# The values of a gated recurrence: turned in 32 by 32 blocks by VectorE when projected, and stored as rows of tokens

## The chip, the cores and the metric

The kernel runs on one core of one Trainium2 chip. The metric is the device time of one execution in microseconds. Each version is run several times on the chip and the median is given; one further execution is recorded by the hardware profiler.

## What is computed

One layer of a hybrid decoder: width 1024, a sequence of 1024 tokens behind 16 learned meta tokens (1040 in all), everything in fp32. In the reference:

```python
h = h + 0.5 * swiglu(rms_norm(h, ffn1_norm), ffn1_w_in, ffn1_w_out)
u = rms_norm(h, mix_norm) @ w_in
hq, hf, hi, hg, sq, sk, sv = split(u)
o_hg = hgrn2(hq, hf, hi, hg, lb, hgrn_out_norm)      # 4 heads, keys and values of 128
o_sb = stick_breaking(sq, sk, sv, sb_q_norm, sb_k_norm)  # 8 heads of 64
h = h + concat(o_hg, o_sb) @ w_out
h = h + 0.5 * swiglu(rms_norm(h, ffn2_norm), ffn2_w_in, ffn2_w_out)
```

The change concerns `hgrn2`, a recurrence over tokens with a matrix S as its state in each head:

```python
# S_t = diag(f_t) S_{t-1} + (1 - f_t) i_t^T ;  o_t = S_t^T q_t ;  y = RMSNorm_head(o) * silu(g)
f = lb + (1 - lb) * sigmoid(f_raw);  k = (1 - lb) * sigmoid(-f_raw);  q = silu(q_raw);  v = i_raw
# in blocks of 128 tokens: scores inside a block, the state between blocks
```

The value v (the i of the formula) enters in two places: in the product of the scores inside a block with v, and in the update of the state, keys by v. Both sum over tokens.

## The kernel before

**Layout.** Activations are kept turned: the features lie on the partitions, the tokens along the row. Matmuls with weights are made of three products of high and low fp32r parts (`product`, lines 243 to 254), so that a step of `wo` or `proj` is a triple of matmuls of lines 250, 251 and 252.

**The recurrence's columns.** `hgrn_fill` (line 1085) projects, for each of the 4 heads, the columns of v, f, q and g in this order (line 1079). For v and f the tokens are cut in the four pieces of `PIECES` (line 31), for q and g in two halves. A piece is taken out of PSUM by `use` (line 1093): for v by a copy on ScalarE into a staging tile (line 1101; four tiles `st` take turns, line 1091), for f by two sigmoids on ScalarE and two operations on VectorE (1103 to 1109), for q and g by a sigmoid and a product (1112, 1113). Then SP stores the tile in DRAM (`hg_v`, `hg_f`, `hg_k`, `hg_q`, `hg_g`; lines 1110 and 1114), each with features as rows and tokens along the row. Of v, f and q the second half of the tokens is stored in reversed order.

A first part of these columns is woven into the projections of the stick-breaking heads; 76 steps are spread by `braid` (line 1609) over the stick-breaking attention (scores, log-weights `wu` and `wm` subtracted on VectorE at line 1535, TensorE transposes of them through `flip` at line 1417); what is left runs beside the first pieces of the heads.

**The heads.** `hgrn_attend` (line 1138) is a generator, one for each head; each `yield` gives the planner a cost on TensorE and a wait. Its pieces are:

- loads from DRAM (lines 1149 to 1152): vT first (the whole v of the head, 128 by 1040), then KB, QA, F and the meta parts KM and FM; the decay products over 1, 2, 4 ... 64 tokens on GpSimd (line 1168);
- nine transposes on TensorE of vT, through `flip` (lines 1172 to 1176): one of the 16 meta tokens, copied to vm by VectorE, and two groups of four blocks of 128, each copied to vr by ScalarE. vr and vm have tokens on the partitions, as the products with v want them;
- the scores KB by QA inside blocks (line 1187), the diagonal taken out by VectorE (1189), QA multiplied by F (1190);
- seven levels (line 1204), each with a copy of KB to KP on ScalarE (1208), a product on TensorE into the banks `lvl` (1213), its selection into `attn` (VectorE's copy_predicated at 1220 for the first five, ScalarE copies at 1230 for the last two), and two pairs of products with the decays on VectorE (1243);
- the transposes of the keys (1248 and 1255, `km` and `knp`), copied out to kms and kn; kn lies in vT's tile. Then the load of g into KB's tile (1258);
- the state: `s` (1262), seven products `up` of kn and vr (1269), and the chain over blocks on VectorE (1272). km, knp, s, up and the later `onp` share two PSUM banks (`tr`);
- the outputs `op` (1282, 1286), their norm (squares on ScalarE 1291, root 1293, reciprocal and product on VectorE 1294 to 1296, the product written into kn), and the transposes back `onp` (1302), gated by g (1305) and split in high and low parts `oH` (1310, 1311).

Tiles of a head have three buffers each, so head 3 reuses those of head 0: its loads wait until head 0 has let them go.

**Order.** TensorE's order is written by hand, by `weave` (line 1639): it keeps a clock, adds the costs that the generators and the fill give, and takes a head's next piece when its wait has passed. The fill is first the rest of the columns, beside which only the first pieces of heads 0 to 2 run (line 2123), then `mix_out` (1579), the products of the stick-breaking half of o with w_out (`wo`), which need oT, loaded at line 2151, and the weights wh and wl, loaded at line 221. There are three lanes: heads 0 and 3, head 1, head 2 (2176, 2177). The order on VectorE, ScalarE and SP is decided by the scheduler.

Of the kernel before, what the change touches and what calls it, by code (L numbers as in the profile page):

```python
# [11 lines left out]
F32 = mybir.dt.float32  # L12
# [8 lines left out]
P = 128  # L21
D = 1024
KT = D // P
SEQ = 1024
META = 16
T = META + SEQ
# [1 line left out]
EPS = 1e-6  # L28
HALVES = [(META, 512), (META + 512, 512)]
CHUNKS = [(META + 512, 512), (0, 264), (264, 264)]  # L30
PIECES = [(0, 264), (264, 264), (528, 256), (784, 256)]
LEVELS = [1, 2, 4, 8, 16, 32, 64]
NEG = -1e30

# [6 lines left out]
class Block:  # L41
# [1043 lines left out]
    def hgrn_fill(self, xh, xl, pool, dst):  # L1085

        nc = self.nc
        plan, cols = self.heads_plan, self.columns_of_heads()

        def staged(n):  # L1090
            return pool.tile([P, 512], F32, tag="st", name="st", bufs=4)[:, :n]

        def use(kind, h, ps, c0, n):
            s = slice(c0, c0 + n) if kind in "vf" else slice(c0 - META, c0 - META + n)
            t = staged(n)
            if c0 >= HALVES[1][0] and kind != "g":
                ps = ps[:, ::-1]
                at = s.start + HALVES[1][0] + T - 2 * c0 - n
                s = slice(at, at + n)
            if kind == "v":  # L1100
                nc.scalar.copy(t, ps)
            elif kind == "f":
                k = staged(n)
                nc.scalar.activation(t, ps, AF.Sigmoid)
                nc.scalar.activation(k, ps, AF.Sigmoid, scale=-1.0)
                nc.vector.tensor_scalar(
                    t, t, self.lbc[:, h : h + 1], self.lb[:, h : h + 1], ALU.mult, ALU.add
                )
                nc.vector.tensor_scalar_mul(k, k, self.lbc[:, h : h + 1])
                nc.sync.dma_start(dst["k"][h, :, s], k)  # L1110
            else:
                nc.scalar.activation(t, ps, AF.Sigmoid)
                nc.vector.tensor_mul(t, t, ps)  # L1113
            nc.sync.dma_start(dst[kind][h, :, s], t)

        def weights(i):
            return self.col_tile(self.a["w_in"][0], cols[i])

        kept = {"next": None}

        def part(i, ci, c0, n, half):
            if ci == 0 and half == 0:
                kept["w"] = kept["next"] or weights(0)
                kept["next"] = weights(i + 1) if i + 1 < len(plan) else None
            if half == 0:
                kept["ps"] = self.proj_bank(n)
            self.product(
                kept["ps"], kept["w"], xh, xl, c0, n, range(4 * half, 4 * half + 4)
            )
            if half == 1:  # L1130
                use(*plan[i], kept["ps"], c0, n)

        for i, (kind, _) in enumerate(plan):
            for ci, (c0, n) in enumerate(PIECES if kind in "vf" else HALVES):
                for half in range(2):
                    yield 12 * (n * 0.42 + 13), lambda a=(i, ci, c0, n, half): part(*a)

    def hgrn_attend(self, h, pool, src, oH):
# [3 lines left out]
        nc = self.nc  # L1142

        def tile_of(name, n):
            return pool.tile([P, n], F32, tag=name, name=name, bufs=3)

        QA, KB, F, vT = (tile_of(x, n) for x, n in (("QA", SEQ), ("KB", SEQ), ("F", SEQ), ("vT", T)))
        KM, FM, TM = (tile_of(x, META) for x in ("KM", "FM", "TM"))
        for t, x in ((vT, src["v"][h]), (KB, src["k"][h][:, META:]), (QA, src["q"][h]),
                     (F, src["f"][h][:, META:]), (KM, src["k"][h][:, :META]),  # L1150
                     (FM, src["f"][h][:, :META])):
            nc.sync.dma_start(t, x)
        vr = tile_of("vr", SEQ).rearrange("p (c d) -> p c d", d=P)
# [4 lines left out]
        vm, kms = (  # L1158
            pool.tile([META, P], F32, tag=x, name=x, bufs=3) for x in ("vm", "kms")
        )  # L1160
        ss, sq = tile_of("ss", 8), tile_of("sq", P)
        where = [0, 1, 2, 3, 7, 6, 5, 4]
        decays, at = [F], 0
        for n in LEVELS:
            nb = 512 // (2 * n)
# [2 lines left out]
            nc.gpsimd.tensor_mul(decays[-1], tk[:, :, 0], tk[:, :, 1])  # L1168
            at += 2 * nb
        yield 0, 4000  # L1170

        ps = self.flip(vT, [(0, META)])
        nc.vector.tensor_copy(vm, ps[:META, 0, :])
        for q in range(2):
            ps = self.flip(vT, [(META + (4 * q + j) * P, P) for j in range(4)])
            nc.scalar.copy(vr[:, 4 * q : 4 * q + 4, :], ps)
        yield 960, 500

        def strided(x, offset, *dims):
            y = x[:, offset:]  # L1180
            return bass.AP(y.tensor, y.offset, [list(d) for d in (y.ap[0], *dims)])

        for half in range(2):
            ps = self.pz.tile([P, 4, P], F32, tag="z", name="lvl")
            for j in range(4):
                c = slice((4 * half + j) * P, (4 * half + j + 1) * P)
                nc.tensor.matmul(ps[:, j, :], KB[:, c], QA[:, c], start=True, stop=True)
            m = self.ident.unsqueeze(1).broadcast_to([P, 4, P])
# [46 lines left out]
        for i, n in enumerate(LEVELS):  # L1235
            level(i, n)
            nb = 512 // (2 * n)
            for eng, x, x0, x1, t0, t1 in (
# [3 lines left out]
                y = strided(x, x0, (x1, 2), (2 * n, nb), (1, n))  # L1242
# [4 lines left out]
        km = self.ptr.tile([P, P], F32, tag="tr", name="km")  # L1247
        nc.tensor.transpose(km[:META, :], KM, self.ident)
        nc.vector.tensor_copy(kms, km[:META, :])
        kn = vT[:, :SEQ].rearrange("p (c d) -> p c d", d=P)  # L1250
        for q in range(2):
            ps = self.ptr.tile([P, 4, P], F32, tag="tr", name="knp")
            for j in range(4):
                s = (4 * q + j) * P
# [6 lines left out]
        ps = self.ptr.tile([P, P], F32, tag="tr", name="s0")  # L1261
        nc.tensor.matmul(ps, kms, vm, start=True, stop=True)
        nc.vector.tensor_copy(S[:, 0, :], ps)
        for q in range(2):
            ps = self.ptr.tile([P, 4, P], F32, tag="tr", name="up")
            js = [j for j in range(4) if 4 * q + j < 7]
            for j in js:
                c = where[4 * q + j]
                nc.tensor.matmul(ps[:, j, :], kn[:, c, :], vr[:, c, :], start=True, stop=True)
            for j in js:  # L1270
                c = 4 * q + j
# [27 lines left out]
        for half, on in enumerate(outs):  # L1299
            ps = self.ptr.tile([P, 4, P], F32, tag="tr", name="onp")  # L1300
            for j in range(4):
                nc.tensor.transpose(ps[:, j, :], on[:, j, :], self.ident)
            t = attn[half].rearrange("p c t -> p (c t)")
            ps = ps.rearrange("p j t -> p (j t)")
# [383 lines left out]
    def run(self):  # L1688
        nc, tc, a = self.nc, self.tc, self.a
# [20 lines left out]
        with ExitStack() as c0:  # L1710
            with ExitStack() as c1:
# [121 lines left out]
                with tc.manual_schedule(engines={nc.tensor.engine}), ExitStack() as c2:  # L1833
# [46 lines left out]
                    v = [nc.vector] * 2  # L1880
# [204 lines left out]
                with tc.manual_schedule(engines={nc.tensor.engine}):  # L2085
# [20 lines left out]
                    for i, n in enumerate(LEVELS[:5]):  # L2106
                        m = self.masks[:, i, :].rearrange("p (b h r) -> p b h r", h=2, r=n)
# [30 lines left out]
            with tc.manual_schedule(engines={nc.tensor.engine}), ExitStack() as cx:  # L2138
                with ExitStack() as c1:
# [100 lines left out]
                r = self.inv_rms_rows(sums[1], n, px, ppb)  # L2240
# [55 lines left out]
```

## Time and profile before

| | us |
|---|---|
| median of 3 runs | 2004.04 |
| lowest and highest run | 2003.74, 2004.24 |
| the profiled execution, device time | 2002.59 |
| its span in the profile | 2000.7 |
| granted TensorE clock, mean | 0.999 of full speed |

How to read the lines below. Times are in microseconds unless marked ns. PE is TensorE's matmuls, PEld its weight loads (beside PE), DVE is VectorE, ACT ScalarE, POOL GpSimd, SP the engine that issues most DMAs (SPq its queue). L1176 is line 1176 of the kernel before. `out<-in` are the program's names of tiles. A row of a timeline gives start, duration, engine, line, operation, tiles, shapes and count, and in square brackets how long the engine had been idle before, and what ended that. A row of the chain gives start, duration and what ran: the chain is followed back from the last instruction, at each step to what released it. In groups by line, the number after the bar is busy time, then the mean of one in ns, then the engine's idle time just before these instructions with its releasers. Waits are listed as: who <- on what, sum in us, times, longest. DMA rows give the count, the size and the median time from issue to landing. Where a row has three numbers with slashes, they are the least, the median and the greatest duration in ns, followed by the starts of the first and the last.

### The profile page before, as it was taken

What the parts mean: (1) busy time and instruction counts of PE and PEld (TensorE: products, weight loads), DVE (VectorE), ACT (ScalarE), POOL (GpSimd) and SP (SyncE); (2) the same over time, 40 slices, a digit from 0 to 9 for tenths busy, and PEclk for the clock granted to TensorE, in tenths of its full rate; (3) what the DMA queues carried; (4) which work ended last, traced back from release to release, by engine and by line L of the source; (5) the groups of instructions that cost most, each with busy time, mean ns of one, the idle gap of its engine ahead of it and who ended that gap; (6) DMA issues with size and microseconds to landing.
All of it is one profiled execution on the core that took longest, in us unless ns stands there. A gap on an engine that the chain in (4) does not pass through costs nothing.

```text
span 2000.7 us, 30716 instructions
## 1 busy us (share of the span) xinstructions
PE 1956.6 (98%) x10940; PEld 1646.5 (82%) x10940; DVE 1362.6 (68%) x2140; ACT 860.7 (43%) x1731; POOL 455.3 (23%) x604
## 2 busy tenths in 40 slices
PE   7999999999999999999999999999999999999998
PEld 6788888888888888888888978877888888888887
DVE  7977777876677752247777767557566767767774
ACT  6523443334444544456666635433132332344443
POOL 3010100010000003233333331320544644520000
PEclk9999999999999999999999999999999999999999
DMA  7256787758965226445454166665523323268463
GB/s 211 87 160 170 250 269 248 242 184 314 381 197 185 95 88 182 142 137 132 121 149 121 56 254 174 167 223 171 193 95 111 106 95 111 100 262 305 118 199 137
DMA packets 315576, 347.16 MB, mean 174 GB/s; under 512 B 61520, under 2 KB 216656, under 8 KB 315424
## 3 DMA queue, kind: packets, MB, share of 16 engines
q1 hardware_dynamic: 297136, 292.18, 46.5%
q0 software_dynamic: 17248, 53.03, 7.7%
q8 instruction: 86, 1.41, 0.3%
q14 instruction: 66, 0.54, 0.1%
q10 hardware_dynamic: 1040, 0.00, 0.0%
HBM read 233.75 MB, written 111.38 MB: 173 GB/s over the span
## 4 chain that ended last, share of the span: by engine, by line
PE 91%; DVE 4%; DMA 2%; ACT 1%; issue 1%; POOL 0%; SPq 0%; DVEq 0%; ACTq 0%
PE o L723 21%; PE qb L450 17%; PE qc L450 12%; PE qa L450 12%; PE proj L250 5%; PE proj L252 5%; PE proj L251 5%; PE flip L1420 2%; PE wo L250 1%; PE wo L251 1%; PE wo L252 1%; PE mq L992 1%; PE lvl L1213 1%; PE oacc L1490 1%; PE oacc L1492 1%; PE z L1556 1%
## 5 line engine op out<-in xcount | busy, mean ns | idle before, releaser
L450 PE MATMUL qb<-T,wh 128*128 128x512 f32 x1056 | 344.5, 390 | 1.3 <-ACT T L310 0.8
L450 PEld LDWEIGHTS qb<-T,wh 128*128 128x128 f32 x1056 | 198.1, 188 | 46.5 <-issue 2.5
L450 PE MATMUL qa<-B,wh 128*128 128x512 f32 x696 | 226.6, 390 | 0.3 <-ACT B L826 0.2
L250 PE MATMUL proj<-xh,wh 128*128 128x512 f32 (+2 forms) x640 | 216.5, 338 | 0.8 <-DVE st L1113 0.7
L723 PE MATMUL o<-t,w 128*128 128x512 f32 x924 | 212.1, 390 | 0.5 <-DVE u L541 0.5
L252 PE MATMUL proj<-xl,wh 128*128 128x512 f32 (+2 forms) x640 | 209.8, 328 | 0.8 <-DVE xl L1875 0.8
L723 PE MATMUL o<-parts 128*128 128x512 f32 x924 | 209.9, 389 | 0.0
L251 PE MATMUL proj<-xh,wl 128*128 128x512 f32 (+2 forms) x640 | 209.9, 328 | 0.0
L450 PE MATMUL qb<-T,wl 128*128 128x512 f32 x528 | 205.7, 390 | 2.7 <-DVE wl L363 2.7
L723 PEld LDWEIGHTS o<-t,w 128*128 128x128 f32 x924 | 172.7, 188 | 37.7 <-issue 0.6
L723 PEld LDWEIGHTS o<-parts 128*128 128x128 f32 x924 | 173.3, 188 | 36.0
L363 DVE TENSOR_TENSOR wl<-s,wh 128x512 fp32r<-128x512 f32 x160 | 165.5, 1035 | 50.6 <-ACT wh L361 49.7
L361 ACT CAST wh<-s 128x512 fp32r<-128x512 f32 x160 | 99.3, 621 | 189.3 <-PE qb L450 148.0
L450 PEld LDWEIGHTS qa<-B,wh 128*128 128x128 f32 x696 | 130.5, 188 | 27.9 <-DVE B L827 0.5
L361 ACT CAST wh<-raw 128x512 fp32r<-128x512 f32 x120 | 74.4, 621 | 145.8 <-PE qc L450 106.1
L450 PE MATMUL qa<-B,wl 128*128 128x512 f32 x348 | 135.4, 389 | 0.0
L252 PEld LDWEIGHTS proj<-xl,wh 128*128 128x128 f32 x640 | 120.5, 188 | 12.2 <-DVE xl L1875 1.2
L250 PEld LDWEIGHTS proj<-xh,wh 128*128 128x128 f32 x640 | 120.7, 189 | 11.4 <-DVE st L1113 1.2
L251 PEld LDWEIGHTS proj<-xh,wl 128*128 128x128 f32 x640 | 120.6, 188 | 9.1
L450 PEld LDWEIGHTS qb<-T,wl 128*128 128x128 f32 x528 | 99.1, 188 | 23.3 <-DVE wl L363 3.1
L450 PE MATMUL qc<-T,wh 128*128 128x512 f32 x352 | 117.0, 394 | 0.0
L450 PE MATMUL qc<-B,wh 128*128 128x512 f32 x352 | 115.1, 390 | 1.1 <-DVE u L541 1.1
(396 smaller groups left out, 3898.0 us busy)
## 6 DMA issues: line engine op xcount, KB each, us to landing
raw<-in_ffn_w_in_dram SPq DMA_DIRECT2D x176, 256.0 KB, 4.0
raw<-in_ffn_w_out_dram SPq DMA_DIRECT2D x112, 256.0 KB, 4.4
w2in<-both SPq DMA_DIRECT2D x28, 512.0 KB, 3.4
raw<-in_w_in_dram SPq DMA_DIRECT2D x25, 512.0 KB, 4.1
ks<-kD SPq DMA_DIRECT2D x32, 260.0 KB, 4.8
wout<-both SPq DMA_DIRECT2D x16, 512.0 KB, 4.0
wh<-w2in SPq DMA_DIRECT2D x27, 256.0 KB, 3.4
wl<-w2in SPq DMA_DIRECT2D x27, 256.0 KB, 3.3
```

The lines of the kernel that those rows point to most:

```text
L250: nc.tensor.matmul(ps, wh[:, s], xs, start=k == 0, stop=False)
L251: nc.tensor.matmul(ps, wl[:, s], xs, start=False, stop=False)
L252: nc.tensor.matmul(ps, wh[:, s], xl[:, k, c0 : c0 + n], start=False, stop=k == nk - 1)
L361: nc.scalar.copy(hi, src)
L363: nc.vector.tensor_sub(lo, src, hi.bitcast(F32))
L450: nc.tensor.matmul(ps, a[:, k, :], b[:, k, :], start=start and k == 0 and i == 0, stop=k == 3 and i == 2, skip_group_check=True,)
L723: nc.tensor.matmul(banks[bank][m], y[:, m * P : (m + 1) * P], z, start=start and at == 0 and e == 0, stop=q == nq - 1 and e == 2, skip_gro ...
L992: nc.tensor.matmul(ps[at : at + 32, at_g, :], self.xm[:, 4 * h + k, :], got[i, h][:, k, :], start=h == 0 and kk == 0, stop=h == 1 and kk = ...
L1213: nc.tensor.matmul(ps[:, :, c, :], kp[:, P * c : P * c + P], strided(QA, P * c + n, (512 - n, 2), (2 * n, nb), (1, n)), start=True, stop=True,
L1420: self.nc.tensor.transpose(ps[:m, j, :], src[:, s0 : s0 + m], self.ident)
L1490: nc.tensor.matmul(o[:, c], vj, w[0], start=j == 0, stop=False, skip_group_check=True)
L1492: nc.tensor.matmul(o[:64, c], vj[:, :64], w[1], start=False, stop=end, skip_group_check=True)
```

## The change

A v piece is still copied from PSUM into a staging tile by ScalarE. Then VectorE transposes its 32 by 32 blocks into a second staging tile: 128 features by 256 tokens at once. In the result, row r of partition group b holds the token r of each block, along the row, with 32 features of group b side by side. Four DMAs, one for each group of 32 partitions, store it to `hg_v`, which is now of tokens by features: each has 32 partitions with 8 runs of 32 floats (128 bytes), 32 KB in all. The first piece has the 16 meta tokens besides, with a transpose of 128 by 32 and four stores of 16 by 32 of its own; for that the cut of `PIECES` is now 272 and 256 instead of 264 and 264. A head loads vm (16 by 128) and vr (128 by 8 by 128, in runs of 512 bytes) straight from `hg_v`, after its other loads. The transposes of vT on TensorE, the copies to vm and vr, and the `yield` behind them are gone. kn has a tile of its own.

```diff
-PIECES = [(0, 264), (264, 264), (528, 256), (784, 256)]
+PIECES = [(0, 272), (272, 256), (528, 256), (784, 256)]
...
             if kind == "v":
                 nc.scalar.copy(t, ps)
+                y = staged(n)
+                at = [(n - 256, s.start + n - 256, 8, 32)] + [(0, 0, 1, META)] * (c0 == 0)
+                for x0, to, nb, m in at:
+                    turned = y[:, :256]
+                    if m < 32:
+                        turned = pool.tile([P, 32], F32, tag="st0", name="st0")
+                    nc.vector.transpose(turned, t[:, x0 : x0 + 32 * nb])
+                    for b in range(4):
+                        rows = dst["v"][h, to : to + m * nb, 32 * b : 32 * b + 32]
+                        nc.sync.dma_start(
+                            rows.rearrange("(j r) d -> r j d", r=m),
+                            turned[32 * b : 32 * b + m].rearrange("r (j d) -> r j d", d=32),
+                        )
+                return
...
-        QA, KB, F, vT = (tile_of(x, n) for x, n in (("QA", SEQ), ("KB", SEQ), ("F", SEQ), ("vT", T)))
+        QA, KB, F, kn, vr = (tile_of(x, SEQ) for x in ("QA", "KB", "F", "kn", "vr"))
+        kn, vr = (t.rearrange("p (c d) -> p c d", d=P) for t in (kn, vr))
...
-        for t, x in ((vT, src["v"][h]), (KB, src["k"][h][:, META:]), (QA, src["q"][h]),
+        for t, x in ((KB, src["k"][h][:, META:]), (QA, src["q"][h]),
                      (F, src["f"][h][:, META:]), (KM, src["k"][h][:, :META]),
-                     (FM, src["f"][h][:, :META])):
+                     (FM, src["f"][h][:, :META]), (vm, src["v"][h, :META]),
+                     (vr, src["v"][h, META:].rearrange("(c t) d -> t c d", t=P))):
             nc.sync.dma_start(t, x)
...
-        ps = self.flip(vT, [(0, META)])
-        nc.vector.tensor_copy(vm, ps[:META, 0, :])
-        for q in range(2):
-            ps = self.flip(vT, [(META + (4 * q + j) * P, P) for j in range(4)])
-            nc.scalar.copy(vr[:, 4 * q : 4 * q + 4, :], ps)
-        yield 960, 500
...
-        kn = vT[:, :SEQ].rearrange("p (c d) -> p c d", d=P)
...
-        hgD = {x: self.dram.tile([4, P, T if x in "vfk" else SEQ], F32, name=f"hg_{x}")
-               for x in "vfkqg"}
+        hgD = {x: self.dram.tile([4, P, T if x in "fk" else SEQ], F32, name=f"hg_{x}")
+               for x in "fkqg"}
+        hgD["v"] = self.dram.tile([4, T, P], F32, name="hg_v")
```

In the order of TensorE as the changed program builds it, nothing moves up to the end of the stick-breaking attention. After it, the score product of head 0 stands where its transposes of vT stood. The key transposes of heads 0 and 1 follow each other directly, so do their `s` and `up`; the outputs `op` of two heads follow with a few `wo` between; and more `wo` are left for the end, after the last transposes `onp`.

More of the change, by code (lines that the diff above doesn't have):

```diff
@@ L1145, in tile_of @@
             return pool.tile([P, n], F32, tag=name, name=name, bufs=3)
-        QA, KB, F, vT = (tile_of(x, n) for x, n in (("QA", SEQ), ("KB", SEQ), ("F", SEQ), ("vT", T)))
+        QA, KB, F, kn, vr = (tile_of(x, SEQ) for x in ("QA", "KB", "F", "kn", "vr"))
+        kn, vr = (t.rearrange("p (c d) -> p c d", d=P) for t in (kn, vr))
         KM, FM, TM = (tile_of(x, META) for x in ("KM", "FM", "TM"))
-        for t, x in ((vT, src["v"][h]), (KB, src["k"][h][:, META:]), (QA, src["q"][h]),
+        vm, kms = (
+            pool.tile([META, P], F32, tag=x, name=x, bufs=3) for x in ("vm", "kms")
+        )
+        for t, x in ((KB, src["k"][h][:, META:]), (QA, src["q"][h]),
                      (F, src["f"][h][:, META:]), (KM, src["k"][h][:, :META]),
-                     (FM, src["f"][h][:, :META])):
+                     (FM, src["f"][h][:, :META]), (vm, src["v"][h, :META]),
+                     (vr, src["v"][h, META:].rearrange("(c t) d -> t c d", t=P))):
             nc.sync.dma_start(t, x)
-        vr = tile_of("vr", SEQ).rearrange("p (c d) -> p c d", d=P)
         at8f = tile_of("attn", SEQ)
@@ L1157, in hgrn_attend @@
         Ts = tile_of("Ts", SEQ - 8)
-        vm, kms = (
-            pool.tile([META, P], F32, tag=x, name=x, bufs=3) for x in ("vm", "kms")
-        )
         ss, sq = tile_of("ss", 8), tile_of("sq", P)
```

## Prediction

> **What bounds the kernel now.** The page comes first. Its first line gives the span, then busy time by engine, and further down the chain that ended last, by engine.
>
> ```profile
> span 2000.7 us, 30716 instructions
> ...
> PE 1956.6 (98%) x10940; PEld 1646.5 (82%) x10940; DVE 1362.6 (68%) x2140; ACT 860.7 (43%) x1731; POOL 455.3 (23%) x604
> ...
> PE 91%; DVE 4%; DMA 2%; ACT 1%; issue 1%; POOL 0%; SPq 0%; DVEq 0%; ACTq 0%
> ```
>
> TensorE is busy 98% and carries 91% of the chain, so an instruction off TensorE is time off the end wherever TensorE is what ends last. That is a matter of stages, so the table of busy time by windows is next. The projections of the recurrence lie between 840 and 1150 us, and the four heads between 1172 and 1320 us. Columns: window, its length, then busy us and count of PE, PEld, DVE, ACT, POOL, the granted clock, DMA share, GB/s.
>
> ```profile
> 840.00:930.00 90.00, 87.82 (x575) 76.24 (x575) 47.15 (x77) 52.05 (x122) 32.95 (x43) 1.00 0.41 130
> ...
> 1010.00:1090.00 80.00, 79.55 (x580) 71.94 (x579) 57.49 (x93) 53.20 (x136) 27.64 (x44) 1.00 0.51 141
> ...
> 1172.00:1196.70 24.70, 21.09 (x147) 18.45 (x146) 18.59 (x26) 8.26 (x13) 15.39 (x42) 1.00 0.95 355
> 1196.70:1225.40 28.70, 25.18 (x156) 21.69 (x155) 25.59 (x41) 12.96 (x27) 3.73 (x5) 1.00 0.62 156
> 1225.40:1253.30 27.90, 27.14 (x200) 24.14 (x199) 16.44 (x42) 16.06 (x49) 7.91 (x12) 1.00 0.68 195
> 1253.30:1291.00 37.70, 34.39 (x213) 29.21 (x211) 21.56 (x33) 17.30 (x52) 13.16 (x17) 1.00 0.63 143
> ```
>
> Two pictures. While the columns are projected, TensorE is busy 97.6% (87.82 of 90) and 99.4% (79.55 of 80), and VectorE has 43 and 22 us of slack. When heads 0 to 2 begin, TensorE idles 3.6 us of 24.7 and 3.5 of 28.7, with VectorE busy 25.59 of 28.7 in the second. The timeline of VectorE shows that its row of work from 1177 on leaves no gap until 1212.97, after which it waits for a product:
>
> ```profile
> 1177.01 0.69 DVE L1189 TENSOR_TENSOR attn<-lvl,ident 128x512 f32<-128x512 f32 x1 [3.51 <-PE lvl L1187]
> ...
> 1212.28 0.69 DVE L1243 TENSOR_TENSOR KB<-KB,Ts 128x512 f32<-128x512 f32 x1
> 1215.04 0.69 DVE L1243 TENSOR_TENSOR QA<-QA,Ts 128x512 f32<-128x512 f32 x1 [2.07 <-PE lvl L1213]
> ```
>
> So most of the flips that go lie in a stretch where VectorE sets the pace, not TensorE.
>
> **What goes.** The groups by line, with their forms apart, and the chain give the flips, the copies out of PSUM and their price. Columns: count, then busy us and mean ns.
>
> ```profile
> L1420 PE MATMUL flip<-ident,vT 128*128 128x128 f32 x32 | 4.8, 278 | 0.7 <-ACT vr L1176 0.7
> L1420 PE MATMUL flip<-ident,vT 128*16 128x128 f32 x4 | 1.1, 272 | 0.0
> ```
> ```profile
> L1173 DVE COPY vm<-flip 16x128 f32<-16x128 f32 x4 | 1.1, 276 | 4.8 <-PE flip L1420 4.8
> ```
> ```profile
> L1176 ACT COPY vr<-flip x8: 577/586/596, 1172.8 to 1256.0; 128x512 f32<-128x512 f32 x8
> ```
> ```profile
> 1172.14 1.14 PE flip L1420 x9
> ...
> 1255.37 0.47 ACT vr L1176
> ```
>
> The mean of 278 ns counts the pipeline; nine in a row advance the chain 1.14 us, 0.127 each. 36 flips are 4 x 1.14 = **4.6 us** of TensorE. 27 of them (3.4 us) stand between 1172 and 1188, nine (1.1 us) after 1253. The 27 count although VectorE is the bound there: in the built order, head 0's score product takes the flips' place at 1172, and it is what VectorE waits for:
>
> ```profile
> 1175.91 1.95 PE L1187 MATMUL lvl<-QA,KB 128*128 128x128 f32 x16
> ```
>
> It starts up to 1175.91 - 1172.0 = 3.9 us earlier, so VectorE's row does too; I credit no more than the 3.4 of work removed. This needs KB and QA by 1172; ScalarE's first copy out of KB, which waited for its load, ran at 1169.63, so they are there, and the 520 KB load of vT no longer stands ahead of them.
>
> ```profile
> 1169.63 0.87 ACT L1208 COPY KP<-KB 128x512 f32<-128x512 f32 x1 [2.42 <-DMA KB<-hg_k]
> ```
>
> Three waits of TensorE hang on the same instructions or come late by the same shift:
>
> ```profile
> 1179.08 0.66 PE L1420 MATMUL flip<-ident,vT 128*128 128x128 f32 x4 [0.68 <-ACT vr L1176]
> ...
> 1213.15 0.50 PE L250 MATMUL wo<-oT,wh 128*128 128x512 f32 x1 [1.69 <-DMA wh<-wout]
> ...
> 1258.28 0.63 PE L1302 MATMUL onp<-ident,vT 128*128 128x128 f32 x4 [0.79 <-DVE vT L1296]
> ```
>
> The first (0.7) goes with the vr copy. The third (0.8) ends in the normalization, whose squares on ScalarE stood behind vr copies (0.47 us of the chain at 1255.37, another after it); it goes. The second (1.7) is a weight transfer: heads' work is moved ahead of w_out products there, so I take it as gone; if not, it comes back whole. **Gains: 4.6 + 0.7 + 0.8 + 1.7 = 7.8 us.**
>
> **What is added.** VectorE gets 16 transposes of 128x256 and four of 128x32. Only the form of 128x512 is in the trace:
>
> ```profile
> L1037 DVE STREAM_TRANSPOSE xts<-xrow 128x512 f32<-128x512 f32 x16 | 11.3, 704 | 0.9 <-DMA xD<-xts 0.5 <-DMA xrow<-in_x_dram 0.4
> ```
>
> Between nothing and 704 ns I take half, 0.35, as the size is half, and 0.1 for the small ones: 16 x 0.35 + 4 x 0.1 = 6.0 us (11.6 at the upper end), between 859 and 1127, where VectorE has the slack above. Cost: nothing, with TensorE's 97 to 99% as the cover; what is queued behind a waiting transpose is rival C.
>
> The stores become four of 32 KB in runs of 128 B per piece (80 in all with the meta rows) for 16 of 132 or 128 KB. The nearest rows are the stores of turned x, 128-byte runs too, against those of before:
>
> ```profile
> xD<-xts SPq DMA_DIRECT2D x64, 64.0 KB, 3.8
> ...
> vT<-hg_v SPq DMA_DIRECT2D x4, 520.0 KB, 5.2
> ...
> hg_v<-st SPq DMA_DIRECT2D x8, 132.0 KB, 2.3
> ```
> ```profile
> L1040 SPq DMA_DIRECT2D xD<-xts x64: 302/575/2537, 115.9 to 359.8; - x64
> ```
> ```profile
> 859.81 9.91 SPq L1114 DMA_DIRECT2D hg_v<-st  x4
> ```
>
> Four issues of 0.575 are 2.3 us of SP per piece, landing 3.8 us later. Now four stores of 0.32 us lie spread over 9.9 us of SP's row at 859.81, so 9.2 fit there. The loads of the next column's weights stand behind them on SP and move back by at most that, less than the column of four pieces by which they are ahead. I cost it at nothing; the staging tiles are rival E. The Trainium skill, page "DMA: Bandwidth & Descriptors", section Specifications, speaks against this form: a transfer needs 512 B for line rate, and below that the DMA engine reads, changes and writes back. The trace agrees in direction, 3.8 us for half the bytes that took 2.3; by that rule only rival E gets likelier.
>
> The loads: vr comes in 512-byte runs, the last of a head's instead of vT as the first. The vT loads took 5.2 us; the first reader of vr is the state product:
>
> ```profile
> 1229.81 1.83 PE L1269 MATMUL up<-vr,vT 128*128 128x128 f32 x14
> ```
>
> That is 60 us after the load of KB had landed (1169.63); with ten times the duration it would still be in time, so it costs nothing.
>
> **What is given back.** The built order puts pieces of several heads closer together, since a step of the planner with pauses is gone. Rows that give the prices:
>
> ```profile
> 1231.01 2.71 DVE L1272 SCALAR_TENSOR_TENSOR F<-F,Ts,up 128x128 f32<-128x128 f32 x7 [0.71 <-PE up L1269]
> ```
> ```profile
> 1284.62 1.13 PE L1213 MATMUL lvl<-QA,KP 128*128 128x128 f32 x8 [0.77 <-DVE QA L1243]
> ```
> ```profile
> 1249.10 4.72 DMA KB<-hg_k
> ```
> ```profile
> 1227.02 0.59 ACT L1256 COPY vT<-knp 128x512 f32<-128x512 f32 x1 [0.22 <-PE knp L1255]
> ```
>
> - State products of two heads follow each other without w_out work between. They share two banks of PSUM, and the second head's need the first's chain of 2.71 us on VectorE, which begins 0.71 after a product: 2.71 + 0.71 less the 1.3 us of TensorE's 1.83 left beside it, **2.1**.
> - Key transposes of two heads likewise: two bank copies of 0.59 on ScalarE less 0.3 of TensorE's work, **0.9**.
> - The outputs of two heads come as 16 products each with only 6 to 12 w_out ones between: **0.5** for a bank (an estimate between 0 and the 2.1 above).
> - Head 0 ends later in the order, so head 3's load of KB (4.72 us), which reuses its tile, starts about 1.5 later and TensorE meets head 3's scores earlier: **1.4**.
> - One more level of head 3 with a single w_out triple beside it, like the row at 1284.62 (0.77 plus a start): **0.9**.
>
> Together 5.8. Sum: -7.8 + 5.8 = **-2.0 us**. Nothing given back is -7.8; all of it and the 1.7 again is -0.3, and each of the five could be half as much again: +2.6.
>
> **The rivals.** *B, full gain.* The orders are only what the planner thinks; w_out work runs ahead, and the waits above overlap instead of adding. Then 4.6 to 7.0 us go: 1997.0 to 1999.4. For it speaks TensorE's 27.14 of 27.9 us in the third window; against it the two heads back to back.
>
> *D, covered anyway.* VectorE's gapless row is not shortened because something else (the loads at 355 GB/s in the first window) sets its start, and the shift is idle: 0, so 2004.0.
>
> *C, slower: VectorE's order.* A transpose waits for ScalarE's copy, and behind it on VectorE stand the subtractions for the stick-breaking weights that TensorE's flips wait for:
>
> ```profile
> PE flip L1420 <- DVE wu L1535: 2.7, 6, 0.7
> PE flip L1420 <- DVE wm L1535: 1.5, 3, 0.6
> ```
>
> These waits are tight already (nine, 0.7 the longest). If each of the 16 pieces adds up to 0.7, that is 11.2 - 2.0 = +9.2; at 0.5, +6: 2010 to 2013. It decides from (4 + 2.0)/16 = 0.38 us a piece on. Against it: TensorE's row of work has other products between.
>
> *E, slower: the staging tiles.* Four tiles take turns, and a v piece now holds two, the second until its stores land. Head 0's pieces are close:
>
> ```profile
> 859.41 0.38 ACT L1101 COPY st<-proj 128x264 f32<-128x264 f32 x1 [0.85 <-PE proj L252]
> 863.21 0.38 ACT L1101 COPY st<-proj 128x264 f32<-128x264 f32 x1 [0.87 <-PE proj L252]
> 866.16 0.37 ACT L1101 COPY st<-proj 128x256 f32<-128x256 f32 x1 [1.75 <-PE proj L252]
> 869.00 0.37 ACT L1101 COPY st<-proj 128x256 f32<-128x256 f32 x1 [2.47 <-PE proj L252]
> ```
>
> Two pieces are 5.8 to 6.8 us; copy, transpose, four issues and landing are 0.4 + 0.35 + 2.3 + 3.8 = 6.9. Some pieces come late by up to 1, and by 2.7 if the landing is slower; three such make +8.1 - 2.0, about 2009.
>
> **How the numbers follow.** The profiled execution took 2002.59 us, 1.45 under the median of 2004.04; I take differences off the median. Forecast 2004.04 - 2.0 = 2002.0 us, chance 0.50 (its own range 1999.5 to 2006.6); B 0.20; D 0.12; C 0.10; E 0.08. The range from 1997.0 to 2009.0 leaves out C and the ends of B and E, some 0.15. A measurement of this kernel tells about 0.2%, 4 us, from no change. Faster by that (under 2000.0): B and 0.03 of the forecast, 0.23. Slower (over 2008.05): C and E, 0.18. Within: 0.59.
>
> **What would show it.** Right: no flips of vT; head 0's score product near 1172 and VectorE's gapless row from about 1173; TensorE's waits for the state chain near 1230 to 1240 that sum to 2 us or more; TensorE as busy from 840 to 1150 as before, with transposes near 0.35 us. Wrong: longer waits of flips for wu and wm (C), of ScalarE's copies for hg_v stores (E), a score product that waits for loads (D), or none of the waits on the state chain (B). The sum fails most easily in the five returns, each of which is read from an order and not from a run.

## The result

| | us |
|---|---|
| kernel before, median of 8 runs of this comparison | 2003.89 (2001.74 to 2005.48) |
| changed kernel, median of 8 runs | 2009.8 (2006.66 to 2010.6) |
| changed to before | 1.0027, 95% interval 1.0017 to 1.0038 |
| changed kernel, profiled execution and its span | 2010.49, 2008.8 |

The change makes the kernel slower, by 0.27% or 5.4 us (3.4 to 7.6), above the forecast range of 1997.0 to 2009.0. A repeat (run e9 below) gave 1.0031 (1.0021 to 1.0041).

The page of the changed kernel: its span, the busy times and the chain by engine.

```profile
span 2008.8 us, 30743 instructions
...
PE 1958.5 (97%) x10904; PEld 1647.3 (82%) x10904; DVE 1364.3 (68%) x2156; ACT 858.2 (43%) x1723; POOL 456.2 (23%) x604
...
PE 90%; DVE 5%; DMA 2%; ACT 1%; issue 1%; POOL 0%; SPq 0%; DVEq 0%; ACTq 0%
```

TensorE has 36 matmuls fewer (10904 for 10940). It is busy 1.9 us longer all the same (1958.5 for 1956.6), since stretches of this execution ran at a lower clock (0.95 in stage A below), but the span is 8.1 us longer: most of the loss is waiting. VectorE's share of the chain has grown from 4 to 5%. The windows of the columns, where the transposes and stores are added, and the groups and DMA rows of what is new there:

```profile
840.00:930.00 90.00, 87.80 (x576) 76.53 (x575) 47.95 (x79) 50.78 (x118) 34.11 (x44) 1.00 0.45 133
...
1010.00:1090.00 80.00, 79.43 (x576) 71.82 (x574) 58.98 (x99) 51.90 (x134) 28.85 (x44) 1.00 0.53 141
```
```profile
L1108 DVE STREAM_TRANSPOSE st<-st 128x256 f32<-128x256 f32 x16 | 7.0, 440 | 7.5 <-ACT st L1101 7.4
L1108 DVE STREAM_TRANSPOSE st<-st 128x32 f32<-128x32 f32 x4 | 0.7, 169 | 0.0
```
```profile
hg_v<-st SPq DMA_DIRECT2D x64, 32.0 KB, 1.7
```

TensorE is as busy as before (87.80 for 87.82, 79.43 for 79.55). VectorE's added work is 7.7 us, and a store of 32 KB in 128-byte runs lands after 1.7 us. Nothing is lost here. To find where it is lost, the stretch of the heads is cut at four events that both kernels have: the first projection after the stick-breaking attention, the first w_out product, the key transpose `km` of head 0, and the first w_out product after the last `onp`; it ends where the last 2,887 matmuls begin, in the second feed-forward part, the same number in each kernel. The first event's rows, before and after:

```profile
1160.84 0.39 PE L250 MATMUL proj<-xh,wh 128*128 128x512 f32 x1
```
```profile
1163.50 0.40 PE L250 MATMUL proj<-xh,wh 128*128 128x512 f32 x1
```

The profiled execution of the changed kernel is 2.7 us late here. That comes from code that the change doesn't touch: after TensorE's first 3,000 matmuls, at 532 us, it is already 2.7 us late, and the columns add nothing to it (more in the last section). The windows of the four stages, A to D, first of the kernel before, then of the changed kernel; columns as in the prediction, PE busy being the first number after the length:

```profile
1160.80:1196.70 35.90, 32.29 (x195) 27.43 (x196) 24.45 (x68) 10.50 (x17) 17.28 (x44) 1.00 0.89 327
1196.70:1225.40 28.70, 25.18 (x156) 21.69 (x155) 25.59 (x41) 12.96 (x27) 3.73 (x5) 1.00 0.62 156
1225.40:1305.20 79.80, 74.10 (x494) 64.18 (x493) 43.39 (x89) 39.84 (x124) 23.06 (x31) 1.00 0.65 166
1305.20:1345.20 40.00, 39.64 (x183) 32.59 (x182) 22.10 (x40) 11.95 (x23) 9.47 (x15) 1.00 0.72 256
```
```profile
1163.50:1199.40 35.90, 32.31 (x184) 28.07 (x184) 28.23 (x72) 8.48 (x13) 19.15 (x44) 0.95 0.94 317
1199.40:1225.50 26.10, 24.58 (x154) 21.14 (x153) 23.56 (x39) 14.50 (x33) 2.88 (x4) 1.00 0.59 157
1225.50:1309.10 83.60, 71.87 (x462) 60.79 (x460) 39.57 (x83) 36.56 (x114) 21.66 (x31) 0.98 0.61 159
1309.10:1353.50 44.40, 42.40 (x195) 34.59 (x194) 21.99 (x40) 12.43 (x24) 10.16 (x16) 1.00 0.70 245
```

A takes 35.9 us in both, though 27 transposes are gone from it. B is 2.6 shorter, C 3.8 and D 4.4 longer: 190.0 against 184.4 us. These 5.6 us are about the loss of the medians (5.4). The counts say more: in D TensorE has 12 matmuls more to do (195 for 183), which is w_out work that before was done inside A to C, in the waits. In C it has 32 fewer and still takes longer. Idle time of TensorE in all four (length less busy time): 13.2 us before, 18.8 after.

TensorE's waits in the heads, before (the five largest) and after. Columns: who waits on what, us in all, times, longest.

```profile
PE wo L250 <- DMA wh<-wout: 2.5, 2, 1.7
PE onp L1302 <- DVE vT L1296: 2.4, 2, 1.6
PE lvl L1187 <- DVE attn L1220: 2.0, 3, 0.8
PE lvl L1213 <- DVE QA L1243: 1.7, 3, 0.8
PE lvl L1213 <- ACT KP L1208: 1.5, 2, 0.9
```
```profile
PE wo L250 <- DMA wh<-wout: 2.5, 1, 2.5
PE lvl L1195 <- DMA KB<-hg_k: 2.2, 1, 2.2
PE lvl L1221 <- ACT KP L1216: 2.2, 3, 0.9
PE wo L251 <- DMA wl<-wout: 2.0, 2, 1.1
PE lvl L1221 <- DVE QA L1251: 2.0, 4, 0.8
PE onp L1309 <- DVE kn L1303: 1.6, 1, 1.6
...
PE s L1269 <- DVE F L1279: 0.9, 1, 0.9
PE op L1289 <- DVE kn L1303: 0.9, 1, 0.9
...
PE knp L1262 <- ACT kn L1263: 0.4, 1, 0.4
PE up L1276 <- DVE F L1270: 0.4, 1, 0.4
```

New are the wait of head 3's scores for KB (2.2), longer ones of the steps that share PSUM banks between heads (`s`, `up`, `op`, `knp`: 2.6 together, before 0.8), and more waiting for w_out's weights (4.5; before 2.8 with a small one for wl). The chain shows the first of these as a load that takes 5.83 us from its issue:

```profile
1253.87 5.83 DMA KB<-hg_k
```

### The profile page after: what moved, and what is told of

Same layout as the page of the kernel before. It is cut to its first block, busy times and chain, and to the rows that moved or that the text cites. A ratio compares the mean times of both kernels' runs of the same rounds, so it can differ in the third digit from the quotient of the medians.

```text
span 2008.8 us, 30743 instructions
## 1 busy us (share of the span) xinstructions
PE 1958.5 (97%) x10904; PEld 1647.3 (82%) x10904; DVE 1364.3 (68%) x2156; ACT 858.2 (43%) x1723; POOL 456.2 (23%) x604
## 4 chain that ended last, share of the span: by engine, by line
PE 90%; DVE 5%; DMA 2%; ACT 1%; issue 1%; POOL 0%; SPq 0%; DVEq 0%; ACTq 0%
PE o L723 20%; PE qb L450 17%; PE qc L450 12%; PE qa L450 12%; PE proj L250 5%; PE proj L252 5%; PE proj L251 5%; PE flip L1427 2%; PE wo L251 1%; PE wo L250 1%; PE wo L252 1%; PE lvl L1221 1%; PE oacc L1497 1%; PE mq L992 1%; PE oacc L1499 1%
## 5 line engine op out<-in xcount | busy, mean ns | idle before, releaser
L250 PE MATMUL proj<-xh,wh 128*128 128x512 f32 (+3 forms) x640 | 216.5, 338 | 0.8 <-DVE st L1127 0.7
L252 PE MATMUL proj<-xl,wh 128*128 128x512 f32 (+3 forms) x640 | 209.7, 328 | 0.8 <-DVE xl L1883 0.8
L251 PE MATMUL proj<-xh,wl 128*128 128x512 f32 (+3 forms) x640 | 209.7, 328 | 0.0
L363 DVE TENSOR_TENSOR wl<-s,wh 128x512 fp32r<-128x512 f32 x160 | 161.4, 1010 | 50.5 <-ACT wh L361 49.6
```

The lines of the kernel that those rows point to most:

```text
L250: nc.tensor.matmul(ps, wh[:, s], xs, start=k == 0, stop=False)
L251: nc.tensor.matmul(ps, wl[:, s], xs, start=False, stop=False)
L252: nc.tensor.matmul(ps, wh[:, s], xl[:, k, c0 : c0 + n], start=False, stop=k == nk - 1)
L363: nc.vector.tensor_sub(lo, src, hi.bitcast(F32))
```

## The experiments

**Theory O**: what costs the time is not the new path of the values but TensorE's order. The `yield` that went with the transposes was a step of the planner, with a cost of 960 and a wait of 500 (the "pause" below); without it the heads fall into step, two of them reach the same PSUM banks and tiles together, and w_out work that used to fill waits is left for the end. **Rival P**: the path itself costs it (VectorE's transposes in its order, stores in short runs, staging tiles). **Rival N**: the throttle (the clock in A and C of the changed kernel was 0.95 and 0.98) makes most of it. All ratios are to runs of the kernel before on the same chip; each kernel was run 6 to 12 times, the kernel before about 30 times on each occasion.

| run | what | median us | ratio (95%) |
|---|---|---|---|
| e1 | changed, pause kept | 2002.31 | 0.9994 (0.9986 to 1.0003) |
| e2 | before, pause gone | 2012.1 | 1.0045 (1.0030 to 1.0060) |
| e3 | before, transposes and stores added | 2004.15 | 1.0004 (0.9995 to 1.0014) |
| e4 | changed, four KB tiles | 2007.43 | 1.0017 (1.0006 to 1.0028) |
| e5 | changed, three weight tiles | 2004.95 | 1.0004 (0.9994 to 1.0014) |
| e6 | changed, both | 2002.68 | 0.9994 (0.9984 to 1.0004) |
| e7 | changed, pause kept, both | 1999.51 | 0.9978 (0.9968 to 0.9988) |
| e8 | before, both | 2001.77 | 0.9985 (0.9975 to 0.9995) |
| e9 | changed, again | 2008.83 | 1.0031 (1.0021 to 1.0041) |
| e10 | as e7, again | 2000.38 | 0.9983 (0.9974 to 0.9992) |
| e11 | as e7, cost kept, no pause | 2008.53 | 1.0026 (1.0016 to 1.0037) |
| e12 | as e7, longer pause | 2000.57 | 0.9984 (0.9976 to 0.9993) |

**e1, the pause kept.** The changed kernel with the planner's step put back, empty:

```diff
         yield 0, 4000
+        yield 960, 500
```

TensorE's order is then exactly that of the kernel before without the 36 transposes; the matmuls of the two traces follow each other alike.

> The changed kernel, with the planner's step (cost 960, wait 500) kept, though nothing runs in it: TensorE's order is then that of the kernel before without the 36 transposes. Theory O (the order of TensorE's work in the heads costs the time): the waits given back go, and what is left is the gain of the transposes, 1 to 4 us under the kernel before (about 2000 to 2003). Rival P (the new path of the values costs it: stores, loads, VectorE's transposes): no difference to the changed kernel, 4 to 6 us over the kernel before. Rival N (the throttle's short half-speed stretches, which the changed kernel's profile has three of, make most of it): within 2 us of the kernel before.

It took 2002.31 us, 0.9994 of before: the loss is gone, as O has it, and P falls as its cause. N had forecast the same here; it is decided by e2 and e9. The stages A to D of e1:

```profile
1159.20:1193.70 34.50, 29.45 (x170) 24.74 (x169) 24.82 (x65) 6.91 (x11) 16.62 (x44) 1.00 0.96 333
1193.70:1220.60 26.90, 25.09 (x156) 21.72 (x156) 25.68 (x41) 12.93 (x27) 4.27 (x5) 1.00 0.68 175
1220.60:1302.20 81.60, 73.85 (x486) 63.13 (x485) 43.05 (x87) 39.04 (x122) 23.12 (x31) 1.00 0.63 162
1302.20:1342.20 40.00, 39.69 (x183) 32.46 (x182) 22.07 (x40) 11.93 (x23) 9.39 (x15) 1.00 0.72 256
```

A is 1.4 us shorter than before and B 1.8, so TensorE is 3.2 ahead at the end of B, and C, from which nine more transposes are gone, takes 1.8 longer: most of the gain is given back there. 183.0 against 184.4 us: of 4.6 us of removed work 1.4 arrive against this profile of before, and none against that of e3 (below). In A, where 27 transposes are gone, TensorE's waits for VectorE in the scores and levels have grown from 2.8 to 5.1 us: the freed time has become waiting, in the old order too.

**e2, the order alone.** The kernel before, its transposes in place, without the step behind them:

```diff
             nc.scalar.copy(vr[:, 4 * q : 4 * q + 4, :], ps)
-        yield 960, 500
```

Its order on TensorE is that of the changed kernel with the transposes in it.

> The kernel before, with only the planner's step taken out behind the transposes of vT: these stay, TensorE's order is otherwise that of the changed kernel. Theory O: slower than the kernel before by what the changed kernel loses and by the transposes on top, 5 to 9 us (2009 to 2013). Rival P: within 1 us of the kernel before. Rival N: within 2 us.

1.0045: the order alone costs 9 us (6 to 12) with nothing of the new path in the program, as much as the change or more (the intervals overlap). N, which had forecast no more than 2 us, falls as the main cause. Its stages A to D:

```profile
1160.90:1199.30 38.40, 34.15 (x213) 29.24 (x212) 29.37 (x75) 11.83 (x19) 17.17 (x44) 1.00 0.80 290
1199.30:1225.00 25.70, 24.19 (x152) 21.11 (x152) 23.33 (x38) 14.38 (x33) 2.87 (x4) 1.00 0.61 168
1225.00:1308.60 83.60, 72.92 (x470) 62.20 (x469) 39.92 (x84) 37.65 (x116) 21.61 (x31) 0.98 0.60 158
1308.60:1352.30 43.70, 42.48 (x195) 34.73 (x194) 22.17 (x40) 12.57 (x24) 10.32 (x16) 1.00 0.72 250
```

This explains stage A of the changed kernel. The new order makes A 2.5 us longer (38.4 for 35.9). It puts 56 score and level products ahead of the first w_out product in place of 48 (two levels of four products more), and VectorE, which paces them, has 29.37 us to do there in place of 24.45: 4.9 more, while the first score product stands 2.8 us earlier. Taking the transposes out then makes A 2.5 shorter again (35.9; 35.8 in e9, at full clock): the two cancel.

**e3, the additions alone.** The kernel before with the cut of `PIECES`, the transposes and the stores, to a buffer `hg_r` that nobody reads:

```diff
                 nc.scalar.copy(t, ps)
+                y = staged(n)
...
+                    nc.vector.transpose(turned, t[:, x0 : x0 + 32 * nb])
+                    for b in range(4):
+                        rows = dst["r"][h, to : to + m * nb, 32 * b : 32 * b + 32]
```

> The kernel before, with the cut of the pieces, VectorE's 32 by 32 transposes and the stores in 128-byte runs added, to a buffer that nobody reads; the values go the old way. Theory O: no difference, within 1 us, and TensorE as far at 1155 us as in the kernel before. Rival P, as VectorE's order or the staging tiles were to cost: 4 to 9 us slower, with waits of TensorE between 860 and 1130 us.

1.0004, and its interval takes in no change: TensorE's waits for `wu` and `wm` between 840 and 1160 us are those of before, and rivals C and E of the prediction have no case.

```profile
PE flip L1434 <- DVE wu L1549: 2.7, 7, 0.7
PE flip L1434 <- DVE wm L1549: 1.5, 3, 0.5
```

Its heads are those of the kernel before, in the same order, so it also shows how far two profiles of the same heads lie apart. Stage B, and the sum of A to D:

```profile
1199.30:1226.10 26.80, 24.98 (x156) 21.73 (x155) 25.62 (x41) 12.95 (x27) 4.14 (x5) 1.00 0.64 168
...
sum 182.60, PE 170.55 PEld 145.70 DVE 115.25 ACT 75.03 POOL 53.69; mean PE 42.64 PEld 36.42 DVE 28.81 ACT 18.76 POOL 13.42
```

B is 26.8 us here, without the weight wait of 1.7 that stood in the profile of before, and 26.9 in e1: the wait belongs to that one profile and not to the order. So e1's shorter B is no gain of the change, and against this profile e1's stages gain nothing (183.0 for 182.6).

**e4, e5, e6: the rings.** A ring is the set of buffers that a tile takes in turn: a load into it can start only when the oldest buffer is free. The changed kernel with four tiles for KB (e4), three tiles each for w_out's high and low weights (e5), and both (e6); TensorE's order is the changed kernel's in all.

```diff
-            return pool.tile([P, n], F32, tag=name, name=name, bufs=3)
+            return pool.tile([P, n], F32, tag=name, name=name, bufs=3 + (name == "KB"))
...
-                    self.weights("wo", 2, 2, c1)
+                    self.weights("wo", 2, 3, c1)
```

> The changed kernel with four tiles for KB in place of three, so that head 3's keys are loaded at the start and not when head 0 lets its tile go. Theory O, in which each wait of the new order counts: the wait of 2.2 us for that load goes, so 1.5 to 2.5 us under the changed kernel (3 to 4 us over the kernel before). Rival (waits in the heads only move on to the next one, which is a weight transfer): no gain, still 5 us over.

> The changed kernel with three tiles each for the high and low weights of w_out in place of two; order on TensorE unchanged. Theory O2 (the waits that the new order makes for weight transfers are waits for a tile to come free, 4.5 us in its profile, and each counts): 2 to 4 us under the changed kernel, 1 to 3 us over the kernel before. Rival (the transfers themselves are late, or the waits move on): no gain, 4 to 6 over.

> The changed kernel with four tiles for KB and three for each part of the weights. Theory O2: the two gains add, 0 to 2 us over the kernel before; what is left over that is the wait for PSUM banks between heads and the throttle. Rival (waits move on): as with the better of the two alone, 2 to 4 over.

e5 is at 1.0004, its interval apart from both of the changed kernel: the third tile gives back about 5 us (4.6 to 5.4), more than the 2 to 4 expected. So most of the weight waits were waits for a tile to come free. In its profile one is left:

```profile
PE wo L251 <- DMA wl<-wout: 0.7, 1, 0.7
```

e4 lies where O had it, 3.4 us over the kernel before, but it is inconclusive by itself: its interval overlaps those of the changed kernel. The wait for KB is gone from its profile (taken in its slowest run, 2011.31 us), but the next one has grown, that of `onp` from 1.6 to 3.6:

```profile
PE onp L1309 <- DVE kn L1303: 3.6, 2, 2.0
```

With both (e6) the loss is gone, 0.9994, 1 us beyond what was expected.

**e7, e8: pause and rings, and their control.** e7 is e1 with both rings, e8 the kernel before with both rings.

> The changed kernel with the planner's pause kept, four tiles for KB and three for the weights. Theory O2: in the run with the pause alone TensorE was 4.8 us ahead of the kernel before at 1241 us and lost 3.3 of it up to 1291 us, on the load of KB and two weight transfers; with those gone it keeps it: 4 to 6 us under the kernel before. Rival: it is given back all the same, 1 to 2 under.

> The kernel before with four tiles for KB and three for the weights, the control of the last one. Theory O2: its waits for weights are 2.8 us in all, and that for KB is hidden behind the transposes of vT: 1 to 2 us under the kernel before, so that the change with the pause is worth 3 to 4 us where the rings are deep. Rival (the rings are all of the gain): the same time as the run with pause and rings.

e7 is the fastest kernel here, 0.9978 of before, as expected. But the kernel before gains from the rings too: 0.9985, 3.0 us in place of the 1 to 2 expected. The intervals of the two overlap, so the 3 to 4 us that the change was to be worth beside deep rings are not borne out: what it adds (about 1.4 us; 0.4 with e10, the repeat of e7) is not clear of the noise. C of e7 and of e8:

```profile
1224.00:1301.60 77.60, 73.17 (x486) 63.41 (x485) 43.02 (x88) 39.04 (x122) 23.11 (x31) 1.00 0.63 157
```
```profile
1225.90:1303.70 77.80, 73.69 (x496) 64.41 (x494) 43.72 (x89) 39.69 (x124) 23.52 (x31) 1.00 0.62 156
```

With nine transposes fewer, C takes 77.6 for 77.8 us: in these two profiles head 3's transposes are covered by the waits around them. And e6 against e7, the same rings in the two orders, is 0.9994 to 0.9978: the deep rings take about half of the order's cost away, not all.

**e9, e10: repeats** of the changed kernel and of e7, on another chip than e1 to e8.

> The changed kernel once more, on the same chip as the next three: 5 to 7 us over the kernel before by every theory that the runs so far leave.

> The changed kernel with the pause, four tiles for KB and three for the weights, once more on another chip: 3 to 5 us under the kernel before if the first result was no accident.

1.0031 and 0.9983 agree with the first results. The profile of e9 has no slow clock in stages A to D, and they still take 189.0 us:

```profile
sum 189.00, PE 168.65 PEld 142.19 DVE 113.67 ACT 72.08 POOL 54.15; mean PE 42.16 PEld 35.55 DVE 28.42 ACT 18.02 POOL 13.54
```

That is 20.3 us of idle TensorE against 13.2 before, which settles rival N. The waits of TensorE over A to D, summed by what they are for, in us (between heads: `s`, `up`, `km`, `knp`, `op`; levels: the waits of `lvl` for VectorE and ScalarE):

| profile | A to D | idle | w_out's weights | other loads | between heads | levels | `onp` | rest |
|---|---|---|---|---|---|---|---|---|
| before | 184.4 | 13.2 | 2.8 | 0 | 0.8 | 6.4 | 2.4 | 1.0 |
| e3 (heads as before) | 182.6 | 12.0 | 1.4 | 0 | 0.8 | 6.3 | 2.8 | 1.0 |
| e1 (changed, old order) | 183.0 | 14.9 | 2.2 | 0.5 | 0.6 | 8.6 | 2.7 | 0.3 |
| e9 (changed) | 189.0 | 20.3 | 4.0 | 2.9 | 2.6 | 9.0 | 1.6 | 0.3 |
| e7 (e1, deep rings) | 179.6 | 11.6 | 0.9 | 0 | 0.6 | 8.0 | 1.9 | 0.3 |
| e6 (e9, deep rings) | 183.8 | 16.3 | 1.6 | 0 | 2.5 | 8.8 | 3.1 | 0.3 |
| e11 (below) | 186.9 | 17.6 | 2.1 | 1.5 | 2.3 | 9.6 | 1.8 | 0.3 |

From e3 to e1 the order stays and the transposes go, and 2.3 us of it come back as waiting in the levels. From e1 to e9 the program stays and the order changes: other loads (KB above all) grow by 2.4, the steps between heads by 2.0, the weights by 1.8, the levels by 0.4.

**e11, e12: two other orders.** Both are e7 with other numbers in the step: 960 and no wait (e11), 960 and 2500 (e12).

```diff
-        yield 960, 500
+        yield 960, 0       # e11; 960, 2500 in e12
```

> As the last one, but the planner's step kept with its cost of 960 and no wait behind it. Its order is a third one: the state products of head 0 stand alone as before, those of heads 1 and 2 follow each other, and more w_out products are left for the end. Theory O (each pair of heads back to back costs some 2 us, whichever pair it is): 0 to 2 us under the kernel before, like the changed order with the same rings. Rival (the pairs cost nothing; the cost given to the planner, which keeps w_out work flowing, is what matters): 3 to 5 under, like the run with the pause.

> As the run with pause and rings, with a pause of 2500 in place of 500. Its order has no pair of heads back to back either, and differs only about head 3, which comes later by a few w_out products. Theory O: 3 to 5 us under the kernel before. Rival (the gain of that run hangs on its exact order): over 1 us off it either way.

e12 came out as expected (0.9984). e11 did not: 1.0026 with deep rings, although only heads 1 and 2 run in step. Both views of it were wrong. Its stages A and B, and its largest wait:

```profile
1163.10:1204.20 41.10, 33.13 (x200) 28.40 (x200) 32.35 (x77) 9.64 (x15) 18.34 (x45) 1.00 0.92 312
1204.20:1225.20 21.00, 19.50 (x121) 16.79 (x120) 18.68 (x31) 12.03 (x28) 2.67 (x3) 1.00 0.69 171
```
```profile
PE lvl L1222 <- DVE attn L1229: 4.4, 5, 1.2
```

This order puts 64 score and level products ahead of the first w_out product (48 before, 56 in the changed order). A grows to 41.1 us, in which TensorE idles 8.0 (1.5 of it for the load of QA), and the w_out triples that would have filled it come at the end. For A itself one account fits before, e1, e2, e9 and this run to about 1 us: its length goes with the moment at which the row of scores and levels begins and with VectorE's work up to the first w_out product (32.35 us here). But the levels are only 1.6 us of the 6.0 by which e11 idles more than e7; the steps between heads add 1.7, the load of QA 1.5 and the weights 1.2. So a price by pairs of heads is not the right account, and no single wait is: what the orders that lose have in common is w_out work kept for the end (175 or 178 of its matmuls stand after the last `onp`, in place of 163), which these waits could have used. That last reading was not tested by itself.

## Why the prediction was wrong

- **Where it was right.** TensorE in the columns was covered, the transposes and stores cost nothing (0.44 us each for the 0.35 estimated; the stores landed in 1.7 us, not 3.8), so C and E had no case. By the Trainium skill's rule from "DMA: Bandwidth & Descriptors", Specifications, a store in runs below 512 B does not reach line rate. Here 32 KB in 128-byte runs took 1.7 us, as long as 128 KB in long runs had taken before, so by the byte they were slower; whether the short runs or the small size did that, no run here separates, and nothing waited for them.
- **"The 27 count although VectorE is the bound there": this step failed.** VectorE's row did begin earlier, as forecast: the score product stands 11.1 us after the first projection (1174.62 less 1163.50) in place of 15.1 (1175.91 less 1160.84), and VectorE's first product with it 12.6 us after (1176.05 less 1163.50) in place of 16.2 (1177.01 less 1160.84), 3.6 earlier.

```profile
1174.62 1.95 PE L1195 MATMUL lvl<-QA,KB 128*128 128x128 f32 x16
```
```profile
1176.05 1.28 DVE L1197 TENSOR_TENSOR attn<-lvl,ident 128x512 f32<-128x512 f32 x2
```

But I credited 3.4 + 0.7 us without asking what the order then puts into the room. It puts 8 more products paced by VectorE before the first w_out product, with 3.8 us more of VectorE's work (28.23 for 24.45), and A stayed at 35.9. e2 shows the two halves, +2.5 and -2.5. And in the old order (e1), where the row begins only 1.2 us earlier, the levels' waits grow by 2.2 to 2.3 us: A gains 1.4 of the 4.1 credited.
- **"The second (1.7) is a weight transfer ... so I take it as gone": this step failed too.** It is gone at that place, but it is gone in e3 too, where the heads are those of before: I took for a gain what stood in a single profile. And in the new order TensorE meets the same ring of two tiles later: 2.5 and 2.0 us of waits in C and D, where before had 1.1 outside B. e5 shows what the third tile is worth, about 5 us. There, where the ring is deeper, the waits for w_out's weights fall from 4.5 to 0.7.
- **The five returns** were right in their sum, and partly by luck: forecast 2.1 + 0.9 + 0.5 + 1.4 + 0.9 = 5.8; the waits of the profile are 1.3 (`s` and `up`), 0.4 (`knp`), 0.9 (`op`), 2.2 (KB) and some 0.3 more for QA: 5.1, of which 0.8 stood before too. Singly they are off by up to 0.8 to either side, and the waits on the state chain stay under the 2 us that were to show the forecast right. So the sign was lost on the gains. From before to e9, at full clock, TensorE is busy 2.6 us less (4.6 forecast), the waits for vr and of `onp` fall by 0.7 and 0.8 as forecast, but the levels' waits grow by 2.6 (the sum had 0.9, for one level of head 3), and the weights' by 1.2 where 1.7 were to go; the other loads and the steps between heads add 2.9 and 1.8. Together that is 4.4 of the 4.6 us between the two profiles.
- **The rival on the slower side** was the wrong one. I looked for it where things are added and not in what a removed planner step does, though the order was before me. e2, the order alone, is what that rival should have been. That the time came out near E's "about 2009" is no merit of E, whose sum is 2010.1 besides (2004.04 + 8.1 - 2.0).
- **The pure gain** of the removed work is small even in the old order: e1 is 0.9994 and its interval takes in no change. 4.6 us of TensorE instructions were worth 1.4 us at most in the stages; the rest of them stood beside waits for VectorE or for loads. The row that I called gapless from 1177 on is so only from 1183.2: up to there it waits three times, 1.8 us together.

What stays open: what each part of the order's 7 us (e1 against the changed kernel, 0.9994 to 1.0027 and 1.0031) is worth by itself, as the waits move into each other: the table divides them in one pair of profiles, and only the weights (e5) were shown to give time back alone; and whether the change is worth anything at all beside deep rings (e7 and e8 overlap).

## What to carry to other kernels

A step taken out of a hand-planned schedule takes its place in the plan with it: build the order first, and test "old order without the work" and "new order with the work" as two kernels of their own. Where another engine paces a stretch, removing TensorE's instructions there gave little here, and bringing that engine's work forward only brought more of it together (stage A). Deepening the rings that a denser order runs into (here 4 KB a partition for the weights) was worth more than the change.

## What was unexpected in the hardware

The granted clock falls in short stretches. In ten of the fourteen profiles one lies near 75 us, in code that no version changes; the windows of the kernel before and of the changed kernel there, and the stretch itself in the changed kernel:

```profile
60.00:110.00 50.00, 47.32 (x268) 38.25 (x266) 43.82 (x76) 21.82 (x40) 3.16 (x6) 1.00 0.22 70
```
```profile
60.00:110.00 50.00, 47.31 (x259) 38.41 (x258) 42.49 (x74) 21.65 (x40) 2.41 (x4) 0.97 0.23 69
```
```profile
74.10:77.50 3.40, 2.94 (x7) 2.38 (x8) 3.40 (x6) 1.66 (x3) 0.00 (x0) 0.50 0.00 0
```

The clock is at half for 3.4 us, and in the 50 us TensorE starts 9 matmuls fewer. That is about half of the 2.7 us by which the profiled execution was late at stage A; the rest arose before 532 us and was not followed. The first projection of A starts at 1162.4 to 1163.5 us in the ten profiles with this stretch, and at 1159.2 to 1160.9 us in the four without (before, e1, e2, e6). TensorE idles 2.7 us there, up to 74.0 to 74.9 us, in all fourteen, so that pause alone does not set it off. In the heads such stretches stand in the profiles of e2, e4, e5, e7, e10, e11, e12 and the changed kernel, but not in before, e1, e3, e6, e8 or e9; what sets them off was not tried.
